# One decoder layer on one core: when finished blocks are scaled and split, and how early weights are cut

## The chip, the cores and the metric

The kernel runs on one core of a Trainium2 chip. A core has TensorE (PE in the profile; its weight loads are PEld), VectorE (DVE), ScalarE (ACT), GpSimd (POOL) and SyncE (SP), each with its own in-order instruction queue, and 16 DMA engines that they share. The metric is the device time of one execution in microseconds, median of 3 runs.

## The reference

One layer of a decoder over 256 prompt tokens and 8 sample tokens, 264 columns in all, with a model width of 2048 and an inner width of 5504:

```python
h = h + 0.5 * swiglu(rmsnorm(h, norm_ffn1[l]), ffn1_gate[l], ffn1_up[l], ffn1_down[l])
mix, C_f, n_f, m_f, buf = mixing_block(rmsnorm(h, norm_mix[l]), w_in[l], ...)
h = h + mix
h = h + 0.5 * swiglu(rmsnorm(h, norm_ffn2[l]), ffn2_gate[l], ffn2_up[l], ffn2_down[l])
...
y = rmsnorm(h, norm_final)
```

`swiglu(x, wg, wu, wd)` is `(silu(x @ wg) * (x @ wu)) @ wd`. The mixing block is one input projection (7176 columns), four mLSTM heads beside a gated convolution, and one output projection. All weights and states are float32, and each is used once.

## The kernel before

**Layout.** Activations lie with features on the 128 partitions and the 264 tokens along the free dimension: `h` is 16 blocks of 128 x 264, float32. A weight tile of 128 x 128 is the stationary operand.

**A product in three.** Every float32 weight is split into two float16 parts: ACT writes the high half (`high`, L249), DVE the rest (`low`, L257). The normed activations are split in the same way. `three` (L388 to L390) does three float16 matmuls for each 128 x 128 block: high by high, high by low, low by high. A gate or up product over 16 blocks is 48 matmuls. Some blocks are done two at a time with fewer matmuls (`product_pair`, L460, L461, L477, "by seven"), which needs sums of the weights (`weight_sums`, L363 to L367) and of the tokens (`token_sums`, L449) on DVE and `join` (L514 to L524) after it. `GU_SEVEN` and `DOWN_SEVEN` list which units and which down blocks are done so.

**Weights.** `weight_plan` lists all pieces in the order of use. A piece of a gate, up or down matrix has up to `WIDE` = 16 blocks (1 MB, size 2), one of the mixing's two matrices `WK` = 8 blocks (512 KB, size 1; two share one buffer). `fetch` takes the next piece: SP issues its DMA into one of three buffers (four, in the two ffn layers), ACT makes the high half, and `release` makes the low half. Pieces worth `AHEAD` = 6 are fetched ahead, three wide ones. Where `lag` is set, a low half is held until the middle of the running product (`product_wide`) or the next fetch. `product_wide` serves gate, up and down; `product` serves the mixing.

**Time in the program.** All engines' queues are written out by hand. `tick()` counts products, each with a half step in its middle; `at(delta, fn)` puts work at a later tick. So the order in which DVE and ACT meet weights, activations and norms is fixed by these numbers.

**The two ffn layers.** Layer "1" begins with units 0 and 1 together (`products4`, DMA-bound, with the squares of the norm between), then single units from 2. Units 0 to 5 of layer one (0 to 2 of layer "2") multiply the norm's factor in after the product: `zg = pg * norm.r` and `zu = pu * norm.r` on DVE (L987, L993), Silu on ACT (L989), the product of both on DVE (L911), then its split. `watch` with `scalar=True` is a small sum of a PSUM bank on ACT (L661). Meanwhile `norm.renew` makes x again with the factor in it, in four groups of three steps (L826 on DVE, high on ACT, L835 on DVE), `swap` puts it to use, and `form` makes the token sums of it.

**Down products.** In the second half of a layer, each down block's update of h (L1051, or L1026 for pairs) is followed by `done`. In layer one that is `Norm.block` of the mixing's norm: split (`cut`: ACT L249 and DVE L257, tile xm), then the square and its sum on POOL (L844, L848). In layer two it is the square on POOL and `gained` (L1099): ACT multiplies h by the final gain in place. The last two blocks of layer two are done by spans of tokens (`products_by_span`), and after them come the final norm and the output.

Of the kernel before, what the change touches and what calls it, by code (L numbers as in the profile page):

```python
# [16 lines left out]
KB = D // 128  # L17
# [11 lines left out]
WK = 8  # L29
# [22 lines left out]
def spread(b0, b1, n):  # L52
    return [b0 + i for i in range(b1 - b0) if (i + 1) * n // (b1 - b0) > i * n // (b1 - b0)]


GU_SEVEN = {
    "1": spread(7, 21, 8) + spread(22, NFB - 1, 12), "2": spread(4, 21, 10) + spread(22, NFB - 1, 12),
}
DOWN_SEVEN = {
    ("1", 0): (1, 3, 4, 6, 7), ("1", 1): (1, 3, 4, 6),  # L60
    ("2", 0): (1, 3, 4, 6, 7), ("2", 1): (1, 3, 4),
}
PAIRS = sum(len(v) for v in GU_SEVEN.values()) + sum(len(v) for v in DOWN_SEVEN.values())
TH = T // 2

# [29 lines left out]
def weight_plan(a, sevens):  # L95


    plan = []

    def add(key, src, n, m=128):  # L100
        halves = sevens and key[0] in ("in", "out")
        parts = -(-n // (WIDE if sevens and not halves else WK))
        cut = [n * i // parts for i in range(parts + 1)]
        for i, (k0, k1) in enumerate(zip(cut, cut[1:])):
            plan.append((key, src[:, k0:k1, :], k1 - k0, m, 1, i if halves else None))

    def beside(key, rows, n):
        rows = rows.rearrange("g p k m -> p g k m")
        for k0 in range(0, n, WK):
            n_ = min(WK, n - k0)  # L110
            plan.append((key, rows[:, :, k0 : k0 + n_, :], n_, 128, 2, None))

    def ffn(layer, first):
        gu, d = a[f"w{layer}gu"], a[f"w{layer}d"]
        for half, blocks in enumerate(HALVES):
            for j in blocks:
                if sevens and j in GU_SEVEN[layer]:
                    beside((layer, "gu", j), gu[j], KB)
                elif j >= first:
                    add((layer, "g", j), gu[j, 0], KB)  # L120
                    add((layer, "u", j), gu[j, 1], KB)
            b0, b1 = blocks[0], blocks[-1] + 1
            for db in range(0, KB, 2):
                both = d[db : db + 2][:, :, b0:b1, :]
                if sevens and db // 2 in DOWN_SEVEN[layer, half]:
                    beside((layer, "dd", half, db), both, b1 - b0)
                else:
                    for i in range(2):
                        add((layer, "d", half, db + i), both[i], b1 - b0)

    four = a["w1gu"][0:2].rearrange("j g p k m -> p (j g) k m")
    for k0, nk, j0, nj in FIRST:
        plan.append(("four", four[:, j0 : j0 + nj, k0 : k0 + nk, :], nj * nk, 128, nj, None))
    ffn("1", 2)
    add("gates", a["wg"], KB, 64)
    for item in MIX_ORDER:
        for b in mix_blocks(item):
            add(("in", b), a["win"][b], KB)
    half = KB // 2
    for k0 in (0, half):  # L140
        for db in range(2):
            src = a["wout"][db][:, k0 : k0 + half]
            plan.append((("out", db), src, half, 128, 1, db if sevens else None))
    for db in range(2, KB):
        add(("out", db), a["wout"][db], KB)
    ffn("2", 0)
    return plan
# [25 lines left out]
def step(ctx: ExitStack, tc: tile.TileContext, a: dict, shared, bad=None):  # L173
# [89 lines left out]
    def fetch():  # L263

        if not plan:
            return
        key, src, n, m, several, sub = plan.pop(0)
        if half_size and key == "four":
            raw, parts = small()
        elif half_size and sub == 1:  # L270
            raw, parts = (t[:, WK:] for t in pair)
        elif half_size and spool[0] and key[0] in ("1", "2") and next(turn) % 4 == 3:
            raw = spool[0].tile([128, WIDE, 128], F32, tag="wraw", name="wraw", bufs=1)
            parts = wpool.tile([128, WIDE, 2, 128], PART, tag="w", name="w", bufs=4)
        elif half_size:
            raw = wpool.tile([128, WIDE, 128], F32, tag="wraw", name="wraw", bufs=3)
            parts = wpool.tile([128, WIDE, 2, 128], PART, tag="w", name="w", bufs=4)
            pair[:] = raw, parts
            raw = raw[:, :, :m]
        else:  # L280
            raw = wpool.tile([128, WK, 128], F32, tag="wraw", name="wraw", bufs=AHEAD + 1)
            parts = wpool.tile([128, WK, 2, 128], PART, tag="w", name="w", bufs=AHEAD + 1)
            raw = raw[:, :, :m]
        if key == "four":
            n = n // several * several
            raw, parts = raw[:, :n], parts[:, :n]
            nc.sync.dma_start(raw.rearrange("p (f k) m -> p f k m", f=several), src)
            pairs = [(raw, parts[:, :, 0], parts[:, :, 1])]
        elif several > 1:
            raw, parts = raw[:, : several * n], parts[:, : several * n]  # L290
            nc.sync.dma_start(raw.rearrange("p (g k) m -> p g k m", g=several), src)
            pairs = [(raw, parts[:, :, 0], parts[:, :, 1])]
        else:
            raw, both = raw[:, :n], parts[:, :n]
            nc.sync.dma_start(raw, src)
            pairs = [(raw, both[:, :, 0, :m], both[:, :, 1, :m])]
            if half_size and key == "gates":

                pairs = [
                    (raw[:, :, 32 * g : 32 * g + 16], *(both[:, :, i, 16 * g : 16 * g + 16] for i in range(2)))  # L300
                    for g in range(2)
                ]
        lows = []
        for src, h_, l_ in pairs:
            high(h_, src, sw)
            lows.append((l_, src, h_, sw))
        release()
        held.append((lows, (key, parts[:, :, 0], parts[:, :, 1], n, size(key, sub)), parts))
        if not lag[0]:
            release()  # L310
# [103 lines left out]

    def product(key, x, order, m=128, final=False):

        if half_size and key[1] in ("g", "u", "d"):
            return product_wide(key, x, order, final)
        tick()
        ps = bank()[:m, :T]  # L420
        k, half = 0, 0.5
        while k < len(order):
            while room() or not ready:
                fetch()
            hi, lo, n = take(key)
            for i in range(n):
                three(
                    ps, hi[:, i, :m], lo[:, i, :m], x[order[k]], k == 0, k == len(order) - 1
                )
                k += 1  # L430
            if (k < len(order) or lag[0]) and room():
                fetch()
            tick(half)
            half = 0
        return ps
# [337 lines left out]
    class Norm:  # L773
# [63 lines left out]
        def swap(self):  # L837
            self.groups, self.scaled = self.new, True
            self.x = [t[:, i] for t in self.new for i in range(WK)]

        def square(self, kb):
            new = self.acc is None
            sq = t264("acc", 1) if new else t264("sq")
            side.tensor_tensor(sq, h[kb], h[kb], op=ALU.mult)  # L844
            if new:
                self.acc = sq
            else:
                side.tensor_tensor(self.acc, self.acc, sq, op=ALU.add)  # L848
# [44 lines left out]
    def ffn(layer, norm, done, start=None, end=None):  # L893
        with ExitStack() as stack:
# [74 lines left out]
            for half, blocks in enumerate(HALVES):  # L969
                act = {}  # L970
                def block(i, j):
# [5 lines left out]
                    if norm.scaled:  # L977
# [4 lines left out]
                        watch(pu, scalar=True)  # L982
                        activated(j, i, t264("tc"), sg, pu)
                        return
                    watch(pg, scalar=True)
                    zg = t264("ta")
                    nc.vector.tensor_tensor(zg, pg, norm.r, op=ALU.mult)  # L987
                    sg = t264("tb")
                    nc.scalar.activation(sg, zg, AF.Silu)  # L989
                    pu = gate_up(j, "u")  # L990
                    watch(pu, scalar=True)
                    zu = t264("tc")
                    nc.vector.tensor_tensor(zu, pu, norm.r, op=ALU.mult)  # L993
                    activated(j, i, zu, sg)

                for i, j in enumerate(blocks):
                    if half_size and j == (6 if start is not None else 3):
# [9 lines left out]
                        for which in "gu":  # L1007
                            early[2, which] = product((layer, which, 2), norm.x, range(KB))
                    if half_size and j == (3 if start is not None else 1):
                        for n, t in enumerate((1, 1.5, 2.5, 3)):  # L1010
                            for step in range(3):
                                at(t + step / 2, norm.renew, spool[0], 4 * n, step)
                        for g in range(2):
                            at(6 + g + 2 * (start is not None), norm.form, g)
                    lag[0] = half_size and j >= (3 if start is not None else 1)
                    if (j, "g") in early and not first:

# [57 lines left out]
                n1.cut(kb)  # L1075

    nm = Norm("m", V_MIX)
    ffn("1", n1, nm.block, lambda squares: products4(n1.x, ahead, squares))


    n2 = Norm("2", V_N2)
# [18 lines left out]

    def done(kb):
        nf.square(kb)
        gained(kb, slice(0, T))


    def scaled(k0, n, cols, dma):
# [771 lines left out]
```

## Time and profile before

| what | us |
|---|---|
| median of 3 runs | 1816.52 |
| lowest, highest | 1815.74, 1817.52 |
| the profiled execution | 1816.34 |
| its span | 1814.6 |
| PE busy in it | 1780.4 |
| DVE, ACT, POOL busy | 1553.3, 880.2, 142.6 |

| stretch of the span (us) | what runs there |
|---|---|
| 0 to 28 | units 0 and 1 of layer one, with the loading of x |
| 28 to 249 | units 2 to 21 of layer one; the first pair at 102 |
| 249 to 585 | first down half, units 22 to 42 |
| 585 to 698 | second down half of layer one |
| 698 to 1118 | the mixing block |
| 1118 to 1681 | layer two up to its second down half |
| 1681 to 1802 | second down half of layer two |
| 1802 to 1814.6 | end of the final norm, outputs |

How to read it: a row of a timeline has start, length, engine, line, operation, the tiles (out<-in), sizes and count, and in brackets how long the engine idled ahead of it and what ended that. A row of waits has who waited, on what, the sum in us, the count and the longest. A row of the table of windows has the stretch, its length, then for PE, PEld, DVE, ACT and POOL the busy time with the count of instructions, then the granted clock of TensorE (1.00 is full speed), the busy share of the DMA engines and GB/s. In the list of groups, a row has line, engine, operation, tiles, sizes and count, then busy time and the mean ns of one, then idle time ahead of them.

### The profile page before, as it was taken

To read this page: it belongs to the slowest core of one execution; us is meant where nothing else is said; L and a number is where in the kernel's file an instruction comes from. 1 tells how busy PE (TensorE), PEld (TensorE's weight loads), DVE (VectorE), ACT (ScalarE), POOL (GpSimd) and SP (SyncE) were. 2 spreads that over 40 slices of the span, in tenths; PEclk is the share of its full clock that TensorE was granted. 3 is DMA by queue.
4 is the path that set the end of the run, shared out by engine and by line. 5 is a ranking of instruction groups with operands and counts; after the bars stand their busy time and mean duration, and the time that the engine had idled before them with its cause. 6 is when DMAs were issued, how large, how long until landed. Compare 5 with 4: busy or idle time off the path is not lost.

```text
span 1814.6 us, 44307 instructions
## 1 busy us (share of the span) xinstructions
PE 1780.4 (98%) x19368; PEld 1596.7 (88%) x19368; DVE 1553.3 (86%) x2149; ACT 880.2 (49%) x1310; POOL 142.6 (8%) x200
## 2 busy tenths in 40 slices
PE   8999999999999999999999999999999999999986
PEld 7789999999999988888888888899999999999886
DVE  7799988998998888788888866899988999999675
ACT  7444444444444435576566644544444444444333
POOL 1000000000000222222121022000000000000121
PEclk9999999999999999999999999999999999999999
DMA  9456655765665556888887656466655666655543
GB/s 317 150 189 230 205 175 192 241 233 195 207 208 162 182 169 200 298 292 278 278 274 246 229 179 214 161 232 211 207 182 194 220 226 205 217 200 174 188 140 109
DMA packets 99913, 381.43 MB, mean 210 GB/s; under 512 B 10972, under 2 KB 20796, under 8 KB 88960
## 3 DMA queue, kind: packets, MB, share of 16 engines
q1 hardware_dynamic: 90512, 350.52, 57.5%
q0 software_dynamic: 8256, 27.57, 4.3%
q8 instruction: 153, 2.51, 0.5%
q10 hardware_dynamic: 944, 0.45, 0.1%
q14 instruction: 48, 0.39, 0.1%
HBM read 366.72 MB, written 11.78 MB: 209 GB/s over the span
## 4 chain that ended last, share of the span: by engine, by line
PE 79%; DVE 12%; ACT 3%; issue 3%; DMA 2%; POOL 1%; DVEq 0%; SPq 0%; ACTq 0%
PE ps L390 15%; PE ps L389 15%; PE ps L388 15%; PE ps L477 11%; PE ps L460 10%; PE ps L461 10%; DVE w L257 5%; ACT w L249 3%; DVE s L363 1%; DMA raw<-in_w1gu 1%; DVE s L366 1%; DVE t L826 1%; POOL sq L844 1%; DMA wraw<-in_w1gu 0%; DVE r L835 0%
## 5 line engine op out<-in xcount | busy, mean ns | idle before, releaser
L257 DVE SCALAR_TENSOR_TENSOR w<-wraw,w 128x2048 f16<-128x2048 f32 (+4 forms) x425 | 756.2, 1798 | 121.4 <-ACT w L249 120.3
L249 ACT ACTIVATE w<-wraw 128x2048 f16<-128x2048 f32 (+4 forms) x425 | 632.8, 1506 | 118.4 <-PE ps L461 46.0
L390 PEld LDWEIGHTS <-w 128*128 128x128 f16 x3180 | 311.4, 98 | 63.9 <-DVE w L257 17.4
L388 PEld LDWEIGHTS <-w 128*128 128x128 f16 x3180 | 311.7, 98 | 48.6 <-ACT w L249 2.9
L389 PEld LDWEIGHTS <-w 128*128 128x128 f16 x3180 | 311.4, 98 | 46.9
L390 PE MATMUL ps<-r,w 128*128 128x264 f16 x1120 | 309.2, 276 | 1.3 <-DVE w L257 1.3
L389 PE MATMUL ps<-r,w 128*128 128x264 f16 x1120 | 309.2, 276 | 0.7 <-DVE r L835 0.7
L388 PE MATMUL ps<-r,w 128*128 128x264 f16 x1120 | 309.2, 276 | 0.0
L388 PE MATMUL ps<-xm,w 128*128 128x264 f16 x896 | 247.4, 276 | 0.0
L390 PE MATMUL ps<-xm,w 128*128 128x264 f16 x896 | 247.4, 276 | 0.0
L389 PE MATMUL ps<-xm,w 128*128 128x264 f16 x896 | 247.4, 276 | 0.0
L477 PEld LDWEIGHTS <-w 128*128 128x128 f16 x2078 | 199.5, 98 | 28.7 <-ACT w L249 1.1
L461 PEld LDWEIGHTS <-s 128*128 128x128 f16 x2064 | 200.3, 97 | 0.0
L460 PEld LDWEIGHTS <-s 128*128 128x128 f16 x2064 | 198.8, 96 | 0.1
L390 PE MATMUL ps<-a,w 128*128 128x264 f16 (+2 forms) x684 | 180.3, 269 | 8.5 <-DVE w L257 8.4
L388 PE MATMUL ps<-a,w 128*128 128x264 f16 (+2 forms) x684 | 180.3, 269 | 1.0 <-ACT w L249 1.0
L389 PE MATMUL ps<-a,w 128*128 128x264 f16 (+2 forms) x684 | 180.3, 269 | 0.0
L363 DVE TENSOR_TENSOR s<-w 128x2048 f16<-128x2048 f16 (+2 forms) x135 | 159.0, 1178 | 7.3 <-DVE w L257 0.5
L477 PE MATMUL ps<-r,w 128*128 128x264 f16 x1344 | 164.9, 276 | 0.0
L461 PEld LDWEIGHTS <-w 128*128 128x128 f16 x1562 | 152.3, 98 | 4.7 <-DVE w L257 2.6
L460 PEld LDWEIGHTS <-w 128*128 128x128 f16 x1562 | 152.2, 97 | 2.2
L460 PE MATMUL ps<-f,s 128*128 128x132 f16 x1008 | 124.8, 220 | 0.0
(284 smaller groups left out, 2628.1 us busy)
## 6 DMA issues: line engine op xcount, KB each, us to landing
wraw<-in_w2gu SPq DMA_DIRECT2D x86, 1024.0 KB, 5.0
wraw<-in_w1gu SPq DMA_DIRECT2D x82, 1024.0 KB, 5.3
wraw<-in_win SPq DMA_DIRECT2D x112, 512.0 KB, 5.3
wraw<-in_w1d SPq DMA_DIRECT2D x18, 1024.0 KB, 5.2
wraw<-in_wout SPq DMA_DIRECT2D x32, 512.0 KB, 4.7
wraw<-in_w2d SPq DMA_DIRECT2D x16, 1024.0 KB, 5.1
wraw<-in_w2d SPq DMA_DIRECT2D x22, 704.0 KB, 4.0
wraw<-in_w1d SPq DMA_DIRECT2D x20, 704.0 KB, 4.0
```

Of the source, the lines that this page charges most:

```text
L249: nc.scalar.activation(dst, src, AF.Copy, scale=scale)
L257: nc.vector.scalar_tensor_tensor(dst, src, scale, hi, op0=ALU.mult, op1=ALU.subtract)
L363: nc.vector.tensor_tensor(s[:, 0:2], bc, d_.unsqueeze(1).to_broadcast([128, 2, m, 2, 128]), op=ALU.add)
L366: nc.vector.tensor_tensor(s[:, 2], s[:, 1], b_, op=ALU.add)
L388: nc.tensor.matmul(ps, wh, xk[:, 0, :], start=first, stop=False)
L389: nc.tensor.matmul(ps, wh, xk[:, 1, :], start=False, stop=False)
L390: nc.tensor.matmul(ps, wl, xk[:, 0, :], start=False, stop=last)
L460: nc.tensor.matmul(ps, w[0], x[:, 1], start=first, stop=False)
L461: nc.tensor.matmul(ps, w[1], x[:, 0], start=False, stop=last)
L477: nc.tensor.matmul(ps[:, :T], hi[:, i], xs[i][:, 0], start=(k0 + i == 0), stop=False)
L826: nc.vector.scalar_tensor_tensor(self.wide[g][:, i + k], h[k0 + k], gain, self.r, op0=ALU.mult, op1=ALU.mult,)
L844: side.tensor_tensor(sq, h[kb], h[kb], op=ALU.mult)
```

## The change

Six edits. No matmul is added or left out.

1. Layer one's paired units are 9, 11, 12, 14, 16, 17, 19, 20 instead of 8, 10, 12, 13, 15, 17, 19, 20 in the first half.
2. Units 2 to 5 of layer one fetch gate and up weights in pieces of 8 blocks (two for each product, sharing a buffer), and their products run through `product` instead of `product_wide`.
3. `Norm.block_later` takes the place of `block` after layer one's down blocks 0 to 11: the square at once, the high half 1.5 ticks later, the low half 2.5.
4. In `block` (the inner function for early units), the watch of the gate's bank comes after DVE's multiplication, and that of the up product's bank after the activation and its high half.
5. In layer one, the four groups of `renew` start at ticks 1, 2, 3, 4 instead of 1, 1.5, 2.5, 3, and `form` half a tick later. Layer two keeps its ticks.
6. In layer two's second half, `gained` is put two ticks later.

```diff
 GU_SEVEN = {
-    "1": spread(7, 21, 8) + spread(22, NFB - 1, 12), "2": spread(4, 21, 10) + spread(22, NFB - 1, 12),
+    "1": spread(8, 21, 8) + spread(22, NFB - 1, 12), "2": spread(4, 21, 10) + spread(22, NFB - 1, 12),
 }
...
+EARLY = range(2, 6)
...
-        halves = sevens and key[0] in ("in", "out")
+        halves = sevens and (key[0] in ("in", "out") or key[0] == "1" and key[2] in EARLY and key[1] != "d")
...
             parts = wpool.tile([128, WIDE, 2, 128], PART, tag="w", name="w", bufs=4)
+            pair[:] = raw, parts
...
-        if half_size and key[1] in ("g", "u", "d"):
+        if half_size and key[1] in ("g", "u", "d") and (ready or plan)[0][-1 if ready else 5] != (1 if ready else 0):
             return product_wide(key, x, order, final)
...
+        def block_later(self, kb):
+
+            if not half_size or kb >= KB - 4:
+                self.block(kb)
+                return
+            self.square(kb)
+            g, i = kb // WK, kb % WK
+            if i == 0:
+                self.groups.append(
+                    xpool.tile([128, WK, 2, T], PART, tag=f"x{g}", name=f"x{self.tag}{g}")
+                )
+            self.x[kb] = x = self.groups[g][:, i]
+            gain = gains[:, self.col + kb : self.col + kb + 1]
+            at(1.5, high, x[:, 0, :], h[kb], gain)
+            at(2.5, low, x[:, 1, :], h[kb], x[:, 0, :], gain)
...
-                    watch(pg, scalar=True)
                     zg = t264("ta")
                     nc.vector.tensor_tensor(zg, pg, norm.r, op=ALU.mult)
+                    watch(pg, scalar=True)
                     sg = t264("tb")
                     nc.scalar.activation(sg, zg, AF.Silu)
                     pu = gate_up(j, "u")
-                    watch(pu, scalar=True)
                     zu = t264("tc")
                     nc.vector.tensor_tensor(zu, pu, norm.r, op=ALU.mult)
                     activated(j, i, zu, sg)
+                    watch(pu, scalar=True)
...
-                        for n, t in enumerate((1, 1.5, 2.5, 3)):
+                        for n, t in enumerate((1, 1.5, 2.5, 3) if start is None else (1, 2, 3, 4)):
                             for step in range(3):
                                 at(t + step / 2, norm.renew, spool[0], 4 * n, step)
                         for g in range(2):
-                            at(6 + g + 2 * (start is not None), norm.form, g)
+                            at(6 + g + 2.5 * (start is not None), norm.form, g)
...
-    ffn("1", n1, nm.block, lambda squares: products4(n1.x, ahead, squares))
+    ffn("1", n1, nm.block_later, lambda squares: products4(n1.x, ahead, squares))
...
     def done(kb):
         nf.square(kb)
-        gained(kb, slice(0, T))
+        if half_size:
+            at(2, gained, kb, slice(0, T))
+        else:
+            gained(kb, slice(0, T))
```

`start` is given for layer one alone. The else branch and `not half_size` belong to a second copy of the program in float32, which runs only if the watches find a value out of range.

## The prediction

> **What bounds the kernel now.** I read the page first, for the share of each engine, then the waits of PE by stretch, then a table of windows around the stretches that hold waits, and last the timeline of ACT, DVE and POOL in front of each wait.
>
> ```profile
> span 1814.6 us, 44307 instructions
> PE 1780.4 (98%) x19368; PEld 1596.7 (88%) x19368; DVE 1553.3 (86%) x2149; ACT 880.2 (49%) x1310; POOL 142.6 (8%) x200
> ```
>
> PE is the bound: of 1814.6 us only 34.2 are not PE work, and a part of these lies ahead of the first product and behind the last. The diff alters no matmul, so a gain can only come out of PE's gaps. The table of windows shows where they are.
>
> ```profile
> 28.00:80.13 52.13, 46.46 (x388) 38.76 (x389) 45.31 (x58) 31.08 (x53) 3.11 (x1) 0.97 0.51 189
> 80.13:124.61 44.48, 42.80 (x435) 37.63 (x433) 37.01 (x40) 22.36 (x33) 0.00 (x0) 1.00 0.62 213
> 584.75:697.69 112.94, 108.50 (x1261) 96.61 (x1258) 97.76 (x121) 47.40 (x67) 29.77 (x31) 1.00 0.57 182
> 1118.05:1161.70 43.65, 42.96 (x380) 36.99 (x378) 34.12 (x46) 24.74 (x34) 1.53 (x2) 1.00 0.55 186
> 1681.00:1801.70 120.70, 113.42 (x1326) 102.25 (x1324) 84.64 (x116) 48.32 (x70) 22.14 (x27) 1.00 0.46 148
> ```
>
> Length less the first number behind it (PE busy) is the gap: 5.7 us in the early units of layer one, 1.7 up to its second pair, 4.4 in the second half's down products of layer one, 0.7 at the start of layer two, 7.3 in the last down products. Together 19.8 us.
>
> ```profile
> 69.92:73.33 3.41, 0.45 (x3) 0.17 (x4) 2.74 (x3) 3.08 (x5) 0.00 (x0) 1.00 0.00 0
> 73.33:76.75 3.42, 3.42 (x16) 2.34 (x17) 3.25 (x5) 1.30 (x2) 0.00 (x0) 0.50 0.71 228
> ```
>
> A cost hides in the busy time too: behind 3.41 us in which PE worked 0.45, the granted clock (third number from the end) is 0.50 for 3.42 us, which costs half of it, 1.7 us. Everything that the change can reach is thus about 21 us.
>
> **The last down products (scaling two products later).** One such gap, by engine:
>
> ```profile
> 1733.52 0.42 DVE L1051 SCALAR_TENSOR_TENSOR h<-ps,h 128x264 f32<-128x264 f32 x1
> 1734.02 0.63 POOL L844 TENSOR_TENSOR sq<-h 128x264 f32<-128x264 f32 x1 [8.62 <-DVE h L1051]
> 1734.68 0.51 ACT L1099 ACTIVATE h<-h,vecs 128x264 f32<-128x264 f32 x1 [7.44 <-POOL sq L844]
> 1735.10 3.69 ACT L249 ACTIVATE w<-wraw 128x2048 f16<-128x2048 f32 x2
> 1737.03 2.29 DVE L257 SCALAR_TENSOR_TENSOR w<-wraw,w 128x2048 f16<-128x2048 f32 x1 [2.41 <-ACT w L249]
> 1737.05 1.19 PE L477 MATMUL ps<-a,w 128*128 128x264 f16 x9 [0.88 <-ACT w L249]
> ```
>
> The scaling (L1099) writes h in place, so it waits for POOL's square, which waits for DVE's update of h. ACT stands 7.44 us, and the next weights' high half, long landed, is queued behind it; DVE then idles 2.41 us for it, and PE 0.88.
>
> ```profile
> DVE w L257 <- ACT w L249: 28.1, 12, 3.1
> ```
>
> In 1680 to 1800, DVE waits so 12 times, 28.1 us. Two ticks later h and its square are done, except in a pair, where DVE's update of h is itself late; there two pieces' high halves now pass ahead of the scaling, which is enough. Does DVE then keep up?
>
> ```profile
> 1714.24:1754.11 39.87, 35.98 (x452) 32.51 (x449) 30.58 (x37) 13.11 (x16) 6.62 (x9) 1.00 0.48 160
> 1754.11:1773.98 19.87, 17.90 (x156) 15.10 (x156) 14.93 (x30) 10.12 (x16) 7.96 (x10) 1.00 0.55 173
> ```
>
> In both stretches, which hold five of the six gaps, DVE (third engine) has 30.6 and 14.9 us of work against 36.0 and 17.9 of PE. Without its waits it is ahead. No instruction is added; 14 scalings move. Of the 7.3 us I take **6.8**, since a 0.2 us wait in the final sums stays and the judging block of DVE may leave a little. Bounds: 3.4 (half, if pairs still block ACT) to 7.3.
>
> **Layer one's down products (splits later).** The same queueing, without POOL:
>
> ```profile
> ACT xm L249 <- DVE h L1051: 37.3, 8, 7.6
> DVE xm L257 <- ACT xm L249: 8.1, 10, 1.7
> ```
>
> ACT's high half of the normed block waits for h, 8 times for 37.3 us, with weights behind it; then DVE's low half waits for ACT, 10 times for 8.1 us. For blocks 0 to 11 high moves 1.5 and low 2.5 ticks later, and the square goes first. Instruction counts stay. POOL, 29.8 us busy of 113, takes the squares as they come. Blocks 12 to 15 stay as they are, and with them the wait of the gates' product (L541) on the last block:
>
> ```profile
> PE ps L390 <- DVE w L257: 2.3, 2, 1.2
> PE ps L388 <- ACT w L249: 1.0, 1, 1.0
> PE ps L461 <- DVE w L257: 0.5, 1, 0.5
> PE ps L541 <- DVE xm L257: 0.2, 1, 0.2
> ```
>
> The first three, 3.8 us, are waits for weights, and DVE loses more than that (8.1) to ACT ahead of them. Of 4.4 us I take **3.8**; bounds 2.0 (half) to 4.0.
>
> **Early units.** Here DVE sets the pace, in a chain from 28.07 to the low half of block 6's gate weights at 77.71; PE takes that up at 80.13, the first window's end.
>
> ```profile
> 28.07 2.29 DVE L257 SCALAR_TENSOR_TENSOR w<-wraw,w 128x2048 f16<-128x2048 f32 x1 [2.93 <-ACT w L249]
> 77.71 2.29 DVE L257 SCALAR_TENSOR_TENSOR w<-wraw,w 128x2048 f16<-128x2048 f32 x1 [1.12 <-ACT w L249]
> DVE w L257 <- ACT w L249: 4.7, 3, 2.9
> DVE tc L993 <- ACT seen L661: 2.0, 3, 0.7
> DVE ta L987 <- ACT seen L661: 1.8, 1, 1.8
> L257 DVE SCALAR_TENSOR_TENSOR w<-wraw,w 128x1024 f16<-128x1024 f32 x144 | 170.8, 1225 | 29.3 <-ACT w L249 28.9
> ```
>
> DVE waits there 4.7 us for weights' high halves and 3.8 for ACT's watch (L661) to leave a PSUM bank. By term: (1) halves let the first low start some 1.4 us earlier, when half of the 2.93 is cut and the second half waits a little; (2) the watch behind DVE's reading takes away the waits on it in blocks 1 to 3, 3.1 us; (3) the other waits for high halves, 1.8 of the 4.7, shrink by about 1.0, since a high is half as long; (4) in block 0 the wait on the watch becomes a longer one, +1.0, by the mechanism of the next part; (5) the watch now stands between DVE's product and Silu, which costs about +1.0 over three blocks; (6) eight pieces in two cost 2 x 1.225 - 2.29 = 0.16 each, +1.3. Sum -2.2, and I take **2.1** for block 6 being earlier. PE would be able to take 7.4 (5.7 and the clock), but DVE's work does not shrink. The second split by ones (1, 2, 3, 4) only spreads the same work over one more product. The eight added DMAs are SP's, which has little else to issue; no wait of DVE in this stretch is on a DMA, so I put them at nothing. The up product's bank comes free later, by the high half of the activation; no wait of PE is on a bank: nothing too.
>
> ```profile
> 125.00:225.00 100.00, 100.00 (x1194) 91.61 (x1192) 97.60 (x118) 46.75 (x64) 0.00 (x0) 1.00 0.62 208
> ```
>
> The gap of 1.7 us between 80.13 and 124.61 comes of the first pair (block 8) meeting the forms on DVE. With the first pair at block 9 and eight pairs still, one single unit's slack goes first: **1.7** gained. The price is denser pairs: DVE is 97.6% busy from 125 to 225, yet PE had no gap, so the lead it starts with decides. Early part: 3.8; bounds 0 (DVE's chain is no shorter) to 9.
>
> **Layer two's start.** The watch's new place costs here.
>
> ```profile
> 1124.52 0.17 ACT L661 ACTIVATE seen<-ps 128x16 f32<-128x16 f32 x1
> 1124.81 1.28 ACT L989 ACT_TABLE_LOAD   x1
> 1126.97 0.43 DVE L987 TENSOR_TENSOR ta<-ps,rstd 128x264 f32<-128x264 f32 x1
> 1127.43 0.42 ACT L989 ACTIVATE tb<-ta 128x264 f32<-128x264 f32 x1 [1.34 <-DVE ta L987]
> 1129.75 2.29 DVE L257 SCALAR_TENSOR_TENSOR w<-wraw,w 128x2048 f16<-128x2048 f32 x1 [2.35 <-ACT w L249]
> 1154.21 0.27 PE L389 MATMUL ps<-r,w 128*128 128x264 f16 x1 [0.34 <-DVE r L835]
> 1156.07 0.27 PE L389 MATMUL ps<-r,w 128*128 128x264 f16 x1 [0.34 <-DVE r L835]
> ```
>
> Now ACT watches, loads Silu's table in the time in which it waits for DVE, and runs Silu at 1127.43. Then the watch waits for DVE's reading of the same bank (as DVE now waits for the watch), and the load, which stands right in front of Silu, starts behind it: 0.3 + 1.28 on the path to Silu, the weights' high behind it and DVE's low at 1129.75. DVE's chain from there on has waits of ACT on the same path, where 0.35 comes twice more, up to the renewed x on which PE already waits (1154, 1156): 2.3 us later, so PE stands about 3.0 instead of 0.7. Loss **2.3**; bounds 0 (the load is put ahead of the watch) to 4 (with the clock at half behind it).
>
> The Trainium skill, page "ScalarE: Activation LUTs", section "Step-by-step: what each stage is for", says that the load is placed right in front of the activation that needs it, about 2.7 us with its drain. By that price, not the row's 1.28, the loss would be 1.4 greater and the time 1805.9.
>
> **Sum.** -6.8 - 3.8 - 3.8 + 2.3 = -12.1. The profiled execution took 1816.34 (span 1814.6 and 1.7 around it), so 1804.2; the median, 1816.52, is 0.2 above it, so I say **1804.4**.
>
> **Rivals.** *DVE keeps the early part.* The 97.6% speaks for it: DVE ends the pairs when it did and early gain is given back. Then -6.8 - 3.8 + 2.3 = -8.3: 1808. Chance 0.17.
>
> *The wait only moves.* ACT's row of 7.44 us is in a pair, where DVE's own queue keeps the update of h late; a scaling two ticks later can still stand there. Then 3.4 and 2.0 in the down parts: -6.9, 1809.5. Chance 0.15. If it holds everywhere, the change does not do what it says there, and early gain and layer two's loss leave -1.5: 1815. Chance 0.08.
>
> *All gaps close.* -19.8 and the clock's 1.7, less 2 that stay: 1797 to 1799. Against it: DVE's work ahead of 77.71 stays. Chance 0.12.
>
> *The half pieces starve PE (slower).* In lag mode a low is emitted only at the next fetch, behind a tick's renewals.
>
> ```profile
> 64.42 1.25 DVE L835 TENSOR_TENSOR r<-t,r 128x1056 f16<-128x1056 f32 x1
> 65.59 1.70 DVE L826 SCALAR_TENSOR_TENSOR t<-h,whole,rstd 128x264 f32<-128x264 f32 x4
> ```
>
> If eight successive halves (block 4's up to block 6) each wait 1.25 + 1.70, PE loses 23.6 there instead of 7.4: +16.2, with the rest -8.3: 1824. It decides once DVE falls more than the lead of three products behind (eight are 46.46 us of PE, so some 17); that the chain has waits to lose speaks against it. Chance 0.06.
>
> *The clock.* The Trainium skill, page "TensorE: Matmul & The Clock Gate", Part 1, has the clock halve after an idle window of about 3.4 us. The two rows above agree (0.45 busy in 3.41). A stand of 3.0 in layer two could set it off by chance of the window's place: +1.7, 1806, inside my forecast's own range.
>
> **Chances and range.** Forecast (1800 to 1807) 0.42, the rivals as above. The range 1798.5 to 1812 leaves out 1815, 1824 and the best of "all gaps close". A measurement here tells about 0.2%, 3.6 us, from no change: faster 0.86, same 0.08, slower 0.06.
>
> **What would show it.** In the last down products no wait of PE on L257 over 0.5 us and no ACT row L1099 waiting over 1 us for POOL. In layer one's the gaps at 650, 672, 680 gone, DVE's xm waits nearly gone. Block 6's first matmul near 78, granted clock 1.00 throughout, no gap at the first pair. In layer two the table load behind DVE's product and PE's wait on r grown to some 3 us. I am wrong if PE waits appear between 125 and 250, if ACT still stands behind h in pairs, or if the load sits ahead of the watch.

## The result and the profile after

The kernel after takes **1799.77 us** (median of 4 runs, 1799.02 to 1800.72), the kernel before 1816.89 (4 runs, 1815.74 to 1817.52): a ratio of 0.9908, 95% interval 0.9895 to 0.9921. That is 17.1 us faster, where 12.1 were forecast; the time lies in the range (1798.5 to 1812), 4.6 below the predicted one. The profiled execution of after took 1800.72, the slowest of its four, so that the two profiles stand 15.6 us apart.

The page of after has the span and the engines' busy time:

```profile
span 1798.9 us, 44358 instructions
...
PE 1778.2 (99%) x19368; PEld 1598.2 (89%) x19368; DVE 1561.9 (87%) x2157; ACT 884.7 (49%) x1318; POOL 171.0 (10%) x200
```

PE has the same 19368 matmuls. DVE has eight instructions more (the halves) and 8.6 us more work, POOL none more and 28 us more. The table of windows of after, cut at the same matmuls as the one of before (counted from the first); length, then busy time by engine, and the granted clock third from the end:

```profile
27.69:74.31 46.62, 44.71 (x392) 38.09 (x389) 41.97 (x67) 31.73 (x60) 1.82 (x1) 1.00 0.57 201
74.31:118.81 44.50, 42.61 (x434) 37.66 (x432) 42.62 (x42) 22.53 (x34) 0.00 (x0) 1.00 0.72 247
118.81:578.97 460.16, 460.16 (x5511) 421.94 (x5509) 416.83 (x503) 202.68 (x257) 0.00 (x0) 1.00 0.60 201
578.97:687.66 108.69, 107.44 (x1261) 96.98 (x1258) 100.89 (x121) 48.27 (x67) 43.57 (x31) 1.00 0.59 189
687.66:1107.96 420.30, 420.14 (x3651) 364.38 (x3651) 331.95 (x639) 252.90 (x465) 84.63 (x129) 1.00 0.74 250
1107.96:1154.65 46.69, 44.46 (x379) 37.81 (x377) 34.13 (x46) 25.57 (x35) 1.52 (x2) 0.96 0.53 183
1673.95:1786.07 112.12, 112.12 (x1327) 102.66 (x1324) 89.98 (x116) 49.79 (x70) 37.05 (x27) 1.00 0.50 160
```

Length less length gives where the time went. The matmul at 27.69 starts at 27.72 in the kernel before; the prediction's first row begins at 28.00, behind it, so that its length of the early units is 0.3 us short, and so is the "early gain of 5.5 us" in an expectation below.

| stage | before | after | difference | forecast |
|---|---|---|---|---|
| up to the first window | 27.72 | 27.69 | 0.0 | 0 |
| early units, first pair | 96.89 | 91.12 | **-5.8** | -3.8 |
| layer one's down products, second half | 112.94 | 108.69 | **-4.2** | -3.8 |
| layer two's start | 43.65 | 46.69 | **+3.0** | +2.3 |
| last down products | 120.70 | 112.12 | **-8.6** | -6.8 |
| sum | | | -15.6 | -12.1 |

The other stages are the same to 0.1 us. In the last down products PE's busy time is now the whole window: no stop is left.

In the early units, up to the low half of block 6's gate weights (block 6 is unit 6), DVE's waits in the kernel after are, by the view of waits (us in sum, times, longest):

```profile
DVE tc L929 <- ACT tb L1007: 3.1, 3, 2.1
...
DVE w L258 <- ACT w L250: 0.4, 2, 0.2
```

DVE's 4.7 us of waits for high halves are 0.4, and its 3.8 for the watch are gone; in their place it waits 3.1 for Silu (tile tb), which now stands behind the watch. What ended the waits in the last down products:

```profile
DVE w L258 <- ACT w L250: 7.7, 8, 1.2
...
ACT h L1117 <- POOL sq L862: 4.0, 2, 2.4
```

DVE's 28.1 us of waits for ACT's high halves are 7.7. The scaling (L1099, now L1117), which waited 54.1 us for POOL before, waits twice, for 4.0 us in sum, with nothing late behind it. In layer one's down products:

```profile
ACT xm L250 <- DVE h L1069: 25.0, 8, 6.8
...
ACT xm L250 <- DVE h L1044: 6.8, 2, 4.8
...
DVE xm L258 <- ACT xm L250: 1.2, 2, 0.6
...
PE ps L543 <- ACT xm L250: 1.0, 1, 1.0
```

ACT still stands for h (25.0 us behind single blocks, 37.3 before, and 6.8 behind pairs, 19.4 before), but with the next weights already done; DVE's 8.1 us of waits are 1.2. The gates' product, which PE now reaches earlier, stops 1.0 for the last block: about 0.9 of the gain is given back there. Layer two's start, timeline of ACT:

```profile
1117.32 0.18 ACT L663 ACTIVATE seen<-ps 128x16 f32<-128x16 f32 x1 [2.78 <-DVE ta L1004]
...
1117.61 1.28 ACT L1007 ACT_TABLE_LOAD   x1
1118.90 0.42 ACT L1007 ACTIVATE tb<-ta 128x264 f32<-128x264 f32 x1
```

The watch (L663) waits for DVE's product, and the table load and Silu come behind it. The Trainium skill, page "ScalarE: Activation LUTs", section "Step-by-step: what each stage is for", puts the load right in front of its activation, and the rows agree; its 2.7 us they do not show, since Silu starts 1.29 us after the load's start.

### The profile page after: what moved, and what is told of

Same layout as the page of the kernel before. It is cut to its first block, busy times and chain, and to the rows that moved or that the text cites. A ratio compares the mean times of both kernels' runs of the same rounds, so it can differ in the third digit from the quotient of the medians.

```text
span 1798.9 us, 44358 instructions
## 1 busy us (share of the span) xinstructions
PE 1778.2 (99%) x19368; PEld 1598.2 (89%) x19368; DVE 1561.9 (87%) x2157; ACT 884.7 (49%) x1318; POOL 171.0 (10%) x200
## 4 chain that ended last, share of the span: by engine, by line
PE 87%; DVE 8%; issue 2%; ACT 2%; DMA 1%; SPq 0%; DVEq 0%; ACTq 0%
PE ps L392 17%; PE ps L391 17%; PE ps L390 17%; PE ps L479 12%; PE ps L462 11%; PE ps L463 11%; DVE w L258 3%; ACT w L250 1%; DVE t L828 1%; DVE s L365 1%; DVE xm L258 0%; PE ps L1568 0%; DMA raw<-in_w1gu 0%; DVE s L368 0%; DMA wraw<-in_w1gu 0%
## 5 line engine op out<-in xcount | busy, mean ns | idle before, releaser
L258 DVE SCALAR_TENSOR_TENSOR w<-wraw,w 128x2048 f16<-128x2048 f32 (+3 forms) x433 | 762.7, 1780 | 94.7 <-ACT w L250 93.8
L250 ACT ACTIVATE w<-wraw 128x2048 f16<-128x2048 f32 (+3 forms) x433 | 635.5, 1483 | 147.5 <-PE ps L463 54.2
L516 ACT COPY y<-ps 128x132 f32<-128x132 f32 x59 | 15.9, 269 | 227.4 <-PE ps L463 227.4
```

What stands on the lines that cost most here:

```text
L250: nc.scalar.activation(dst, src, AF.Copy, scale=scale)
L258: nc.vector.scalar_tensor_tensor(dst, src, scale, hi, op0=ALU.mult, op1=ALU.subtract)
L516: nc.scalar.copy(y[:, 0], one[:, T : T + TH])
```

## The experiments

Each kernel ran in 4 executions beside the kernel before; times are medians, and the ratio, with its 95% interval, is to the kernel before, which itself lay at 1815.83 to 1816.97 in these sets. The stages hardly touch each other: where the edit is in another stage, a stage's length repeats to 0.1 us, but for the half-clock windows (stretches in which the granted clock is 0.50), some 0.6 us in the early units, and 0.5 us once in the mixing block. So the stage's length says more than the whole time.

### The scaling at once again

```diff
-        if half_size:
-            at(2, gained, kb, slice(0, T))
-        else:
-            gained(kb, slice(0, T))
+        gained(kb, slice(0, T))
```

> The kernel after, with the scaling of a finished down block of layer two put back directly behind its square. Theory (ACT stands in the scaling for POOL's square, the next weights' high half is queued behind it): the scaling waits for POOL some 54 us in sum again (4.0 in the kernel after), PE's waits for weights in the last down products come back with 8.6 us from start to start, 1808.4 us. Rival (the last part got shorter because DVE arrives there with a greater lead from the earlier parts): less than half comes back, 1803 or below.

1808.07 us (0.9952, 0.9935 to 0.9969). Its last down products, and the waits in them:

```profile
1674.39:1795.13 120.74, 114.94 (x1326) 103.14 (x1324) 84.66 (x116) 48.33 (x70) 22.17 (x27) 0.99 0.45 148
```

```profile
ACT h L1117 <- POOL sq L862: 54.1, 10, 13.4
...
DVE w L258 <- ACT w L250: 28.1, 12, 3.1
...
PE ps L392 <- DVE w L258: 4.6, 3, 2.7
```

All 8.6 us are back (120.74 against 112.12), with ACT's and DVE's waits of before to the tenth, although DVE arrived there as in the kernel after. The rival falls. PE's own stops come to 5.8 us here and 7.3 in the kernel before: behind the longest one the clock is at half for 3.4 us (the 0.99 in the row), and PE, slowed by it, stands less at the next two. So the half clock adds nothing to the stage, in which DVE sets the pace at these places.

### The scaling at once, without POOL's squares

```diff
     def done(kb):
-        nf.square(kb)
-        if half_size:
-            at(2, gained, kb, slice(0, T))
-        else:
-            gained(kb, slice(0, T))
+        if kb == 0:
+            nf.square(kb)
+        gained(kb, slice(0, T))
```

> The kernel after, with the scaling at once again, and without POOL's squares of the finished blocks of layer two other than the first (left out: their part of the last norm's sums). The scaling then waits for DVE's update of the block alone. Theory (POOL's square and DVE's late update both hold ACT; layer one's second half, which has no POOL in that chain, lost 4.1): a part comes back, 3 to 5 of the 8.6 us: 1803.5 us. Rival one (the square is the whole of it): nothing comes back, 1799.8. Rival two (DVE's update is the whole of it and the square only follows): 8 come back, 1808.

1799.96 us (0.9914, 0.9897 to 0.9930).

```profile
1672.25:1784.95 112.70, 112.29 (x1326) 102.58 (x1324) 83.22 (x116) 49.01 (x70) 0.63 (x1) 1.00 0.48 158
```

```profile
ACT h L1117 <- DVE h L1069: 22.0, 7, 7.1
DVE w L258 <- ACT w L250: 18.4, 13, 3.1
ACT h L1117 <- DVE h L1044: 13.6, 2, 11.0
```

Only 0.6 of the 8.6 us come back; my theory of two shares (3 to 5) was wrong, rival one is right. ACT still stands 35.6 us for DVE's updates, and DVE 18.4 for ACT, and PE feels next to nothing of it. What made the difference is the last link: in the run above DVE waited 28.1, so 9.7 us more, and PE lost 8.0 of these. (The run also takes 1.4 us of work off DVE, 83.2 for 84.7, far less than the 8.0.) Waits of ACT of up to 11.0 us are harmless here; the step on POOL at their end was not. It takes 0.63 us where nothing slows it; three of the squares of the run above took 1.8 to 1.9 us, beside DVE's low halves. What is not shown is whether the square had to be that step, or whether any 10 us more of waits would have done it: DVE has 84.7 us of work against 112.1 of PE, so about 27 us to spare, which waits of 28.1 use up and waits of 18.4 do not.

### The scaling one product later

```diff
-            at(2, gained, kb, slice(0, T))
+            at(1, gained, kb, slice(0, T))
```

> The kernel after, with the scaling one product later in place of two. Theory (what has to be hidden is POOL's square, 0.63 us, and its place behind DVE's update; without the squares all but 0.6 us came back already): one product is enough, within 0.6 us of 1799.8. Rival (behind pairs, DVE's update is later than that): the scaling waits for POOL over 20 us in sum, PE loses 2 to 4 us, 1802 to 1804.

1799.55 us (0.9905, 0.9889 to 0.9922).

```profile
1672.78:1784.90 112.12, 112.12 (x1327) 102.66 (x1324) 89.24 (x116) 49.33 (x70) 35.80 (x27) 1.00 0.49 160
```

```profile
ACT h L1117 <- POOL sq L862: 22.9, 6, 7.2
DVE w L258 <- ACT w L250: 10.3, 9, 2.3
```

The scaling waits 22.9 us for POOL, as the rival had it, and PE loses nothing: one product is enough.

### Layer one's blocks split at once again

```diff
-    ffn("1", n1, nm.block_later, lambda squares: products4(n1.x, ahead, squares))
+    ffn("1", n1, nm.block, lambda squares: products4(n1.x, ahead, squares))
```

> The kernel after, with both halves of each finished block of layer one made at once again (block in place of block_later). Theory: ACT's high half of the normed block stands for h with weights behind it, DVE's low halves wait for ACT some 8 us again (1.2 in the kernel after), PE loses 5.6 from start to start in place of 1.6 there: 1804.0 us. Rival (the pairs' own DVE work made those gaps, and the later place only helps because the scaling's queue is shorter): 1801 or below.

1804.69 us (0.9934, 0.9918 to 0.9951). The stage, and two windows in it:

```profile
578.66:693.26 114.60, 110.17 (x1261) 97.44 (x1259) 97.86 (x121) 47.40 (x67) 29.75 (x31) 0.99 0.56 184
671.90:675.32 3.42, 1.28 (x18) 0.82 (x15) 2.17 (x4) 3.33 (x4) 1.52 (x2) 1.00 0.39 161
675.32:678.73 3.41, 3.41 (x17) 2.33 (x18) 3.38 (x4) 2.20 (x3) 0.00 (x0) 0.50 0.68 151
```

```profile
ACT xm L250 <- DVE h L1069: 35.9, 8, 7.6
...
DVE xm L258 <- ACT xm L250: 8.1, 10, 1.7
```

108.69 becomes 114.60: the stops of before (0.5 to 1.2 us, at the same three places) with their 4.2 us, and 1.7 more, since here the clock was halved behind a window with 1.28 us of work. In the kernel before the same stops lay otherwise across such windows (the emptiest held 1.72 us of work), and it was not. DVE's waits for ACT are those of before (8.1). The theory holds.

### The watch ahead of DVE's product again

```diff
-                    zg = t264("ta")
-                    nc.vector.tensor_tensor(zg, pg, norm.r, op=ALU.mult)
-                    watch(pg, scalar=True)
+                    watch(pg, scalar=True)
+                    zg = t264("ta")
+                    nc.vector.tensor_tensor(zg, pg, norm.r, op=ALU.mult)
...
+                    watch(pu, scalar=True)
                     zu = t264("tc")
                     nc.vector.tensor_tensor(zu, pu, norm.r, op=ALU.mult)
                     activated(j, i, zu, sg)
-                    watch(pu, scalar=True)
```

> The kernel after, with ACT's watch ahead of DVE's product on the same bank again, in both places. Theory (watch behind the product makes the table load late in layer two, and is worth about 1 us in the early units): layer two's start gives back 3.1 us (wait on r 0.7 in place of 2.2, no half clock), block 6 comes 1.1 later: 1797.8 us. Rival (the watch's order is what the early gain of 5.5 us comes from): early units lose 4 to 5, layer two gains 3.1: 1801.2 us.

1801.59 us (0.9917, 0.9900 to 0.9933).

```profile
74.48:77.89 3.41, 0.70 (x7) 0.36 (x4) 3.38 (x5) 2.38 (x4) 0.00 (x0) 1.00 0.58 240
77.89:81.30 3.41, 2.40 (x12) 1.66 (x13) 3.41 (x3) 2.09 (x2) 0.00 (x0) 0.50 0.39 115
81.30:84.72 3.42, 3.42 (x17) 2.40 (x16) 3.13 (x4) 2.45 (x5) 0.00 (x0) 0.50 0.99 383
1113.09:1156.74 43.65, 42.95 (x379) 36.98 (x377) 34.13 (x46) 24.73 (x34) 1.52 (x2) 1.00 0.55 184
```

```profile
DVE tc L1011 <- ACT seen L663: 4.2, 5, 2.0
...
DVE ta L1005 <- ACT seen L663: 1.4, 1, 1.4
```

Layer two's start is again as before (43.65), so its whole 3.0 us belong to the watch. But the early units lose 5.1 (96.20 in place of 91.12, between the same two matmuls): some 2.2 in stops (block 6's is 3.7 in place of 1.9, an earlier one 1.2 in place of 0.8), and the rest in two windows at half clock. DVE waits 5.6 us for the watch (4.2 of them at the up product's), more than the 3.8 of the kernel before. The rival was right: with the three other edits of the early units in place, 5.1 of the 5.8 us hang on this order. They do not come from it alone, as a run further down shows. Which of the two watches does it was not tried here; the next run moves the first alone.

### The watch behind Silu

```diff
-                    watch(pg, scalar=True)
                     sg = t264("tb")
                     nc.scalar.activation(sg, zg, AF.Silu)
+                    watch(pg, scalar=True)
                     pu = gate_up(j, "u")
```

> The kernel after, with ACT's watch of the gate product put behind Silu and not in front of it. Theory (ACT waits for DVE in the watch and loads the table only behind it, 1.28 us late in both layers): the load runs while ACT waits for DVE, Silu starts some 1.5 to 2 us earlier, in layer two PE's wait on r falls from 2.23 to below 0.7 without a half clock window (-3.1), in layer one block 6's wait of 1.89 closes (-1.5 to -2.0): 1795 us. Rival (the load is issued behind the wait for DVE in any case, being part of the activation): load still right in front of Silu and behind DVE's product, only the watch's 0.3 is saved: 1799 us.

**1795.52 us** (0.9885, 0.9868 to 0.9901). Timeline of ACT in layer two, and the stages:

```profile
1111.62 1.28 ACT L1006 ACT_TABLE_LOAD   x1
1114.38 0.42 ACT L1006 ACTIVATE tb<-ta 128x264 f32<-128x264 f32 x1 [1.48 <-DVE ta L1004]
1114.71 0.17 ACT L663 ACTIVATE seen<-ps 128x16 f32<-128x16 f32 x1
```

```profile
27.72:71.91 44.19, 44.19 (x391) 38.35 (x389) 42.01 (x66) 31.36 (x59) 1.83 (x1) 1.00 0.60 215
71.91:115.87 43.96, 42.61 (x434) 37.66 (x432) 42.08 (x41) 21.98 (x34) 0.00 (x0) 1.00 0.70 246
1105.02:1149.06 44.04, 42.95 (x379) 36.98 (x377) 34.13 (x46) 24.34 (x34) 1.52 (x2) 1.00 0.54 183
```

The load now runs in ACT's wait for DVE and Silu starts when DVE is done, as the theory had it. Layer two's start takes 44.04 in place of 46.69, the early units 88.15 in place of 91.12: 5.6 us by one line moved two lines down. (By the medians it is 4.3, and the two intervals just overlap; of the 5.6, 1.2 are the half clock behind layer two's stop, which the profiled execution of the kernel after had.)

### Whole pieces, the first pair, the ticks

The three other edits of the early units were undone one by one:

```diff
-EARLY = range(2, 6)
+EARLY = range(0)
```

> The kernel after, with the gate and up weights of blocks 2 to 5 of layer one in whole pieces of 2048 again. Theory (halves let DVE's first low half start 2.2 us earlier and shorten its waits for ACT's high halves, against 1.3 us of extra DVE work): block 6's first low half comes some 1.9 us later, its PE wait grows from 1.89 to about 3.8, and a clock window may come on top: 1801.7 to 1805 us. Rival (the watch's order has already taken those waits away, the halves only cost DVE 1.3 us): block 6 comes earlier, 1798.5 us.

```diff
-    "1": spread(8, 21, 8) + spread(22, NFB - 1, 12), ...
+    "1": spread(7, 21, 8) + spread(22, NFB - 1, 12), ...
```

> The kernel after, with the first pair of layer one one place earlier again (block 8 in place of 9). Theory (the first pair met DVE with the forms still to do, and one more single unit gives the slack): a PE wait of about 1.3 to 1.7 us on a weight's low half near the first pair comes back, 1.9 from start to start: 1801.7 us. Rival (the watch's order and the halves, which bring DVE ahead, have closed that gap by themselves): no wait near the first pair, 1799.8 us.

```diff
-... in enumerate((1, 1.5, 2.5, 3) if start is None else (1, 2, 3, 4)):
+... in enumerate((1, 1.5, 2.5, 3)):
...
-                            at(6 + g + 2.5 * (start is not None), norm.form, g)
+                            at(6 + g + 2 * (start is not None), norm.form, g)
```

> The kernel after, with the renewals of layer one at 1, 1.5, 2.5 and 3 products again and the forms at 2 behind them. Theory (the same work of DVE ahead of block 6, only spread otherwise): within 0.5 us of 1799.8. Rival (at the old ticks two renewals of 1.70 and 1.25 us stand in front of one low half): PE's waits on low halves at 58, 65 and 71 us (0.76, 0.64, 0.51) grow by more than 1 us in sum, 1801 us or more.

1800.75, 1799.77 and 1800.29 us (0.9915, 0.9911 and 0.9913), none to be told from 1799.77 by time. In the traces, the matmul that stands at 118.81 in the kernel after comes at 120.02, 118.69 and 118.65. So the halves are worth 1.2 us, below the 1.9 expected; the ticks nothing, as the theory had it; the first pair's place nothing either, against mine. In the kernel with whole pieces, PE's first stop of 1.93 us is back, and costs twice:

```profile
27.43:30.84 3.41, 1.41 (x12) 0.76 (x10) 2.75 (x2) 3.41 (x5) 0.00 (x0) 1.00 1.00 418
30.84:34.26 3.42, 3.42 (x19) 2.26 (x17) 3.32 (x4) 3.42 (x6) 0.00 (x0) 0.50 0.92 323
```

Those 3.8 us (the stop with the 0.2 that each costs beyond its gap, and 1.7 of half clock) shrink to 1.2 up to 118.81, because later stops are shorter for it: block 6's is 0.44 in place of 1.89, where my theory had it grow to 3.8. Then the watch behind Silu without all three edits, by the three diffs above:

> The kernel with the watch behind Silu and the two later places in the down products, but without the halves, the old first pair and the old ticks of the renewals. Theory (the halves are worth 1 us in layer one, the pair and the ticks nothing, as measured with the watch ahead of Silu): 1796.7 us, with PE's first wait of 1.93 at 28 us back and a possible clock window of 1.7 behind it. Rival (with DVE's lead from the watch alone the halves only cost): 1795 us or less.

1801.40 us (0.9915, 0.9898 to 0.9931), as much as 5.9 above the kernel with them; theory and rival were both wrong. PE's waits in its early units, from 27.7 to 123:

```profile
PE ps L392 <- DVE w L258: 6.1, 4, 1.9
...
PE ps L463 <- DVE w L258: 0.8, 1, 0.8
```

Those at the first pair (the 0.8, and one of 1.3 among the four) are back. So the three edits are worth 6.6 us together here (115.87 against 122.43 for that matmul), while in the kernel after each is worth 1.2 or less. That they stand in for one another is the likely reading, but not shown: none was undone alone in this kernel, nor two at a time in the other, and which of pair and ticks does it when the pieces are whole was not tried. The other side is shown: the watch in its best place, without the three, gains only 2.2 of the early units (122.43 against 124.61 in the kernel before), and the three without the watch's new order 0.7 (123.95).

### Block 6 in halves too

```diff
-EARLY = range(2, 6)
+EARLY = range(2, 7)
```

> The kernel with the watch behind Silu (1795.5), and block 6's weights in halves too. Theory (block 6's wait of 1.35 us is for its first whole low half of 2.28 us; half of it takes 1.23): the wait falls to about 0.3 us, 1794.5 us. Rival (DVE sets the pace there, so that the wait moves on to the next piece): 1795.5.

With the watch behind Silu, as in the next run too: **1793.48 us** (0.9874, 0.9858 to 0.9891), 6.3 below the kernel after; the two intervals do not meet.

```profile
71.93:114.37 42.44, 42.44 (x435) 37.75 (x432) 41.24 (x42) 22.82 (x36) 0.00 (x0) 1.00 0.75 251
```

PE stands nowhere in this window, which took 43.96 without the edit, so block 6's wait is gone. Then the same for units 2 to 6 of layer two:

```diff
-... or key[0] == "1" and key[2] in EARLY and key[1] != "d")
+... or key[0] in "12" and key[2] in EARLY and key[1] != "d")
```

> As the run with block 6 in halves, and the single units 2 to 6 of layer two in halves too. Theory (layer two's renewals wait behind whole low halves of 2.29 us with ACT's whole high halves of 1.90 ahead of them; halves shorten both): PE's two waits on r there (0.74 and 0.34) go, 1793.5 us. Rival (the halves only add DVE work, 0.16 us for each piece, ahead of r): no gain, 1794.5 to 1796.

1793.49 us (0.9874, 0.9857 to 0.9890). Layer two's start shrinks from 44.04 to 43.51, too little to be seen in the time: no wait on r is gone but the shorter one (0.34). So there is no gain, as the rival had it; that the time is also the theory's number is luck, since the theory reckoned from 1794.5.

## Why the prediction was right, and where its sum was short

**Last down products** (said 6.8, measured 8.6). The mechanism was right: put back, the scaling at once costs the whole 8.6 again. The term was mis-sized because it counted gaps, 7.3 us of them. The windows show it: the same matmuls had 113.42 us of busy time with six stops and 112.12 without. Matmuls overlap in the stream (460.16 us for 5511 of them in the long window of pairs, 0.08 us each), and one that starts behind a stop shows its whole 0.28 us; so each stop costs about 0.2 us beyond its gap. (For the same reason the 21 us that I took for all that could be reached were too few: the run with block 6 in halves is 23.2 below the kernel before.) And the bounds that I took from "pairs still block ACT" weighed the wrong link: without the square, ACT's waits for DVE's late update of h cost 0.6 us.

**Layer one's down products** (said 3.8, measured 4.2). Right, by the same waits. From the first of the four stops to behind the last, 5.1 us are gained (I had counted 3.9 of gaps and kept 3.8), and 0.9 is given back at the gates' product, which I had not seen.

**Early units** (said 2.1 + 1.7, measured 5.8). Mechanism right in the main, both sizes too small. DVE ends block 6's first low half at 76.53 in place of 80.00, 3.5 us earlier where I had said 2.1. Its waits on the way say why: those for high halves shrank by 4.3 us (4.7 to 0.4), where my terms 1 and 3 had 2.4; its 3.8 for the watch gave way to 3.1 for Silu, 0.7 less, where terms 2, 4 and 5 had 1.1. From there on PE gains another 2.0, said 1.7. That 1.7 was given to the first pair's new place; put back alone, the old place costs nothing. Nor was it only the forms' work: up to 125 DVE stood 11.6 us for high halves in the kernel before, 4.7 of them up to block 6, and 1.0 in all in the kernel after. So the step that failed is that terms were added which are not independent: undone in the kernel after, the watch's order is worth 5.1, since DVE, which is ahead there, then waits 5.6 for the watch, and the halves 1.2. The half clock, 1.7 in the kernel before, went (the clock is 1.00 in both early windows), but I was right to set it aside: PE came to that low half at 80.36 without a stop, 0.36 behind DVE, so at full speed it would have stood for most of the 1.7.

**Layer two's start** (said +2.3, measured +3.0). Right: the load waits behind the watch, and PE's wait on r grows from 0.7 to 2.2 (I said 3.0). Without a half-clock window the stage grows by 1.9 (45.53 in the run with the scaling one product later); the other 1.2 us are the clock, which I had as a rival of 1.7 by chance of the window's place. (The prediction's 1805.9 is 1805.8 when added up, from 1804.4 and 1.4.)

**The rivals and the signs.** DVE did not keep the early part, and the halves did not starve PE. That the wait only moves is true at one product (22.9 us for POOL), but off PE's path, and at two it is nearly gone. The time lies just below my forecast's own range (1800 to 1807), between it and "all gaps close" (1797 to 1799), which I gave 0.12: what it lacks of that are the stop in layer two and those up to block 6. Three signs did not come as I had named them. The scaling still waits twice over 1 us for POOL, and in layer one ACT still stands behind h in pairs (6.8 us), which I had called a sign of being wrong; PE stops for neither, so ACT's waits were the wrong thing to watch. And the clock is not 1.00 throughout, because of layer two's stop.

## What to carry to other kernels

A short step on a third engine, at the end of a long wait, can decide whether the wait reaches the bound engine: before sizing a wait, ask what the next engine would still have stood for without its last link. Where one engine only looks at what another one reads too, put the look behind the work that others wait for, table load included, and not merely behind the other's reading. Gains of edits that each give the same engine a lead are not to be added; and a stop of PE costs more than its gap.

## What the hardware showed unexpectedly

**The clock goes by windows on a fixed grid.** In all 14 profiles every change of the granted clock falls on a multiple of 3.413 us from the first one of its execution. The same stop of 2.23 us in layer two, in the kernel after and in the one with the scaling one product later:

```profile
1143.10:1146.51 3.41, 1.18 (x12) 0.88 (x10) 3.41 (x4) 1.31 (x2) 0.00 (x0) 1.00 0.16 25
1146.51:1149.93 3.42, 3.42 (x18) 2.34 (x17) 2.07 (x3) 2.38 (x4) 0.00 (x0) 0.50 0.73 284
```

```profile
1141.59:1145.00 3.41, 2.19 (x20) 1.76 (x18) 2.57 (x3) 2.81 (x3) 0.00 (x0) 1.00 0.02 7
1145.00:1148.41 3.41, 2.06 (x17) 1.65 (x17) 2.81 (x4) 1.68 (x4) 0.00 (x0) 1.00 0.68 215
```

In the first it lies inside one window, PE works 1.18 us in it, and the next is at half clock; in the second it is cut by a window's end, and nothing happens. Of the eight profiles with this stop four have the half clock, and their stage is 1.0 to 1.3 us longer. Over all runs, within the products, each window of the grid with 1.42 us of work or less was followed by half clock (nine), none with 1.51 or more, unless the clock was halved already; in the last sums two with 1.75 and 1.97 were followed by it too, so that the bound holds for these products alone. The Trainium skill, page "TensorE: Matmul & The Clock Gate", Part 1, has the free-running window of 3413 ns, which agrees; its advice, in "Why this matters for your kernels", to avoid idle gaps over some 3 us is too mild for this kernel, where stops of 2.23 and of 1.93 us (the run with whole pieces) are enough.

**POOL and DVE slow each other.** In the last down products, POOL's squares of before and after (mean ns of one behind the busy time):

```profile
L844 POOL TENSOR_TENSOR sq<-h 128x264 f32<-128x264 f32 x13 | 11.9, 919 | 74.0 <-DVE h L1051 43.3 <-DVE h L1026 30.7
```

```profile
L862 POOL TENSOR_TENSOR sq<-h 128x264 f32<-128x264 f32 x13 | 18.1, 1394 | 50.1 <-DVE h L1069 28.5 <-DVE h L1044 21.6
```

The same squares take half as long again, now that DVE works beside them instead of standing: in the kernel after a square takes 0.63 us while DVE stands and up to 2.60 beside DVE's work on weights. POOL's whole work goes from 22.1 to 37.1 us and DVE's, for the same 116 instructions, from 84.6 to 90.0 (83.2 in the run without the squares). The Trainium skill, page "SBUF — State Buffer", section "Who interferes with whom", says that a DVE instruction with two inputs in SBUF contends with a GpSimd instruction that reads it; the rows agree. It cost PE nothing here, since DVE kept 22 us of slack.
